# Up-projection remainders made by an adding DMA, and ten weight buffers of 1024 columns, in a one-core decoder layer

## The chip, the cores and the metric

The kernel runs on one core of one Trainium2 chip. Its time is the device time of one execution, in microseconds (us); the measure is the median over several runs. The engines are TensorE (PE; PEld is its weight loading), VectorE (DVE), ScalarE (ACT), GpSimd (POOL) and SyncE (SP). SP and ACT issue the DMAs of the kernel before.

## The reference

One decoder layer on a sequence of 512 tokens of width 1024, float32. `D_FF` is 2816, so the up-projection has 2 x 2816 columns.

```
cond = silu(c)
sh1, sc1, g1, sh2, sc2, g2 = split(cond @ ada_w + ada_b)
u = rms_norm(x, mix_pre_g) * (1 + sc1) + sh1
qk_raw, v, o_pre, gates, glu = split(u @ w_in)
qk = silu(causal_dwconv(qk_raw, 4 taps));  h = mlstm_chunkwise(q, k, v, gates)
h = rms_norm(h, ml_norm_g) * sigmoid(o_pre)
y = silu(layer_norm(causal_dwconv(a * sigmoid(gt), 31 taps)))        # a, gt = halves of glu
x = x + g1 * rms_norm(concat(h, y) @ w_out, mix_post_g)
u = rms_norm(x, ffn_pre_g) * (1 + sc2) + sh2
up = causal_dwconv(u @ ffn_up, 3 taps)                               # the stage of the change
a, gt = halves of up
x = x + g2 * rms_norm((silu(gt) * a) @ ffn_down, ffn_post_g)
```

## The kernel before

**Products in three matmuls.** TensorE multiplies in a rounded 32-bit format (`F32R`). To keep float32 accuracy every operand is split in two: `hi` is the value rounded to that format, `lo` the remainder `value - hi`. A product is then `hi*hi + hi*lo + lo*hi`, three matmuls into one PSUM bank (`mm3`, L210). For weights ScalarE writes `hi` (L191) and GpSimd, in some places VectorE, subtracts for `lo` (L192). This is `w_split`; `w_load` fetches 1024 KB of weights (128 partitions x 2048 columns) into one of two raw buffers (pool `raws`) and splits them in four pieces of 512 columns.

**Buffers.** The pieces lie in the pool `wpool`: 20 buffers of 128 x 512 (`WSLOTS = 20`), two for a piece, so ten pieces. A buffer is given out in turn and is free again when the last matmul that reads it is done.

**Stages in the order of the program.** The opening with the first GLU columns, summed up over eight parts of the input as they arrive (`w_part`, `glu_pass`); the rest of the GLU projection; the value and gate columns (`make_v0`); four attention heads with their projections (`qko`, `vo`), with the 31-tap convolution of the other branch on VectorE, ScalarE and GpSimd beside them; the output projection (`mixa`, `mixb`); the up-projection in 22 units of 2 x 128 columns (`up`); the down-projection in seven products of half size (`dn`, Strassen's way of making one product from seven).

**A unit of the up-projection.** 48 matmuls of 512 columns into two PSUM banks of a ring of four; then, per bank, ScalarE and VectorE apply the three taps (`conv3`), ScalarE the silu, VectorE the product `a * silu(gt)`, and for every second unit GpSimd forms sums and ScalarE and VectorE split the result for the down-projection. Beside it run, for 11 of the units, a 1024 KB load of a `w_down` tile `b`, four subtractions on it (VectorE and GpSimd in turn, `weight_sums`) and a 1024 KB store of the result (`spill_t`). The weights of units 0 and 1 are split by VectorE into another pool, those of units 2 and 3 by VectorE into `wpool`; the other 18 units, 4 to 21, go through `w_load` with GpSimd.

**What sets the order.** TensorE and SP execute in the order in which the program is written. For ScalarE, VectorE and GpSimd the build's scheduler picks an order by its own estimates of time; the opening, and the stretch between the output projection and the third up-projection unit, stand in program order on them too. Each engine works through its list in that order and waits where an operand or a buffer isn't ready.

Of the kernel before, what the change touches and what calls it, by code (L numbers as in the profile page):

```python
# [33 lines left out]

WARM = (3, 8, 8, 2)
CVS = 4
WSLOTS = 20
RAWS = 2


# [15 lines left out]
def decoder_layer(ctx, tc, w_glu0, x, c, adaT, vecs, w_glu, w_qko, w_v0, w_vo, w_out, w_up, w_down, out):  # L56
    nc = tc.nc
    V, S, G, PE = nc.vector, nc.scalar, nc.gpsimd, nc.tensor

    const = ctx.enter_context(tc.tile_pool(name="const", bufs=1))  # L60
    slots = ctx.enter_context(tc.tile_pool(name="slots", bufs=SLOTS))
# [120 lines left out]

    def w_split(src, name, pool=None, tag="w", eng=None):

        n = src.shape[1]
        pool = pool or wpool
        hi = pool.tile([P, T], F32R, tag=tag, name=f"{name}h")
        lo = pool.tile([P, T], F32R, tag=tag, name=f"{name}l")  # L190
        S.activation(hi[:, :n], src, AF.Copy)  # L191
        (eng or G).tensor_tensor(out=lo[:, :n], in0=src, in1=hi[:, :n].bitcast(F32), op=ALU.subtract)  # L192
        return hi, lo

    def w_load(view, name, pool=None, tag="w", eng=None):

        n = view.shape[1]
        r = raws.tile([P, 2048], F32, tag="raw", name=name)
        nc.sync.dma_start(r[:, :n], view)
        return [w_split(r[:, a : min(a + T, n)], f"{name}_{a}", pool, tag, eng) for a in range(0, n, T)]  # L200

    def blk(pieces, b):
        hi, lo = pieces[b // 4]
# [135 lines left out]
    rows0 = {}  # L339

    def w_rows(k):
        rows0[k] = adas.tile([P, D], F32, tag="ada", name=f"wglu0_{k}")
        nc.sync.dma_start(rows0[k][:, : G0 * P], w_glu0[k])

    def w_part(k, a, n):
        wk.append(w_split(rows0[k][:, a : a + n], f"wglu0_{k}_{a}"))

    def glu_pass(ps, i, p):
        a, b = ((0, 0), (1, 0), (0, 1))[p]
# [120 lines left out]
    def make_v0():  # L470

        n = DH + GB
        wv = []
        for q in range(0, KT, 4):
            r = raws.tile([P, 2048], F32, tag="raw", name=f"wv0_{q}")
            nc.sync.dma_start(r[:, : 4 * n], w_v0[q // 4])
            wv += [tuple(w[:, :n] for w in w_split(r[:, i * n : (i + 1) * n], f"wv0_{q + i}")) for i in range(4)]
        v_tile(0)
        banks = [mmbank(f"v0_{tt}") for tt in range(NT)]
        for tt, ps in enumerate(banks):  # L480
            ts = slice(tt * P, (tt + 1) * P)
            for k in range(KT):
                mm3(ps[:, :n], (u[k][0][:, ts], u[k][1][:, ts]), wv[k], k == 0, k == KT - 1)
            V.tensor_tensor(out=gz[:, tt, :], in0=ps[:, DH : DH + GB], in1=vcols("gate_b", 0, GB), op=ALU.add)
            S.activation(vs[0][tt][:, :DH], ps[:, :DH], AF.Copy)
# [526 lines left out]

    def up_split(i, r, pool, tag):
        q = len(up_w[i])
        up_w[i].append(w_split(r[:, q * T : (q + 1) * T], f"wup{i}_{q * T}", pool, tag, V))

    NE = 2
    early = []
# [12 lines left out]
            for k in range(KT):  # L1031
                mm3(ps[:, th * HT : (th + 1) * HT], blk(up_w[i], half * KT + k), (u2h[:, th, k, :], u2l[:, th, k, :]), k == 0, k == KT - 1)

    up_w = {0: w_load(w_up[0], "wup0", slots, "t", V)}
    raw1 = raw_up(1)
    send_rows(KT, 2 * KT, nc.sync)
    gs2r = row(1, cvtile, "gs2", nc.sync)
# [96 lines left out]
    for i in range(NF):  # L1134
        if i < NE:
            pa, pg = early[i]
        else:
            pieces = up_w.get(i) or w_load(w_up[i], f"wup{i}")
            if i in AT:
                weight_load(AT.index(i))  # L1140
            if i in (4, 8, 12, 16):
                ada_block(38 + i // 2, last_lo[0])
                ada_block(39 + i // 2, last_lo[0])
            if i == 19:
                ada_done(40, 48)
# [12 lines left out]
        anchor[0] = S.activation(g, g, AF.Silu)  # L1158
        if i % 2 == 0:
            x_, r_, *more = side_parts(f"f{i}") if i >= AT[-1] else [slot(f"f{q}{i}") for q in "xr"]  # L1160
        cs = slice(i % 2 * HT, (i % 2 + 1) * HT)
        V.tensor_tensor(out=x_[:, cs], in0=a[:, :HT], in1=g[:, :HT], op=ALU.mult)
        V.tensor_tensor(out=r_[:, cs], in0=a[:, HT:], in1=g[:, HT:], op=ALU.mult)
        if i % 2:
            y_, q_ = more or [slot(f"f{q}{i}") for q in "yq"]
            G.tensor_tensor(out=y_[:, :HT], in0=r_[:, :HT], in1=r_[:, HT:], op=ALU.add)
            G.tensor_tensor(out=y_[:, HT:], in0=y_[:, :HT], in1=x_[:, :HT], op=ALU.subtract)
            G.tensor_tensor(out=q_[:, :HT], in0=x_[:, :HT], in1=r_[:, :HT], op=ALU.subtract)
            G.tensor_tensor(out=q_[:, HT:], in0=x_[:, HT:], in1=y_[:, HT:], op=ALU.subtract)
            home = [None, None]  # L1170
            if i == NF - 1:
                ends = [adas.tile([P, D], F32R, tag="ada", name=f"f{q}{i}") for q in "xy"]
                home = [(z[:, :T], z[:, T:]) for z in ends]
            af.append(split_f(x_, f"fx{i}", i == 1, home[0]))
            asum.append(split_f(y_, f"fy{i}", i == 1, home[1]))
            j = i // 2
            nc.scalar.dma_start(spill["s34"][:, j * T : (j + 1) * T], q_)
            nc.scalar.dma_start(spill["a22"][:, j * HT : (j + 1) * HT], r_[:, HT:])
        if i - 1 in AT:
            weight_store(AT.index(i - 1))  # L1180
        if i in AT:
            weight_sums(AT.index(i))
# [10 lines left out]
    def product(weights, left, th, hf, name, js=range(JP), start=False, by_tile=JP):  # L1193

        late = []
        for a in range(js.start, js.stop, GJ):
            m = min(GJ, js.stop - a)
            turn_at = at[0] % (RAWS + len(rings))
            r = raws.tile([P, 2048], F32, tag="raw", name=f"{name}_{a}") if turn_at < RAWS else rings[turn_at - RAWS]
            at[0] += 1  # L1200
            nc.sync.dma_start(r[:, : m * T].rearrange("p (j n) -> p j n", j=m), weights(a, a + m))
            for n in range(m):
                j = a + n
                turn[0] += 1
                w = w_split(r[:, n * T : (n + 1) * T], f"{name}_{j}", eng=V if turn[0] % 2 else G)
                if j < by_tile:
                    for q in range(2):
                        piece(left(j), q, w, banks[2 * th + q][hf], start and j == 0, j == js.stop - 1)
                else:
                    late.append((j, w))  # L1210
        return late
# [167 lines left out]
```

## Time and profile before

| what | us |
|---|---|
| median of 3 runs (least, most) | 767.93 (767.7, 768.16) |
| profiled execution, span from first to last instruction | 767.4 |
| median less that span | 0.5 |

The profile is of one execution; it gives its span and no other time of its own. Granted TensorE clock over the span: 0.999 of full speed. A row of a group reads: line, engine, operation, written tile <- read tiles, shapes, count, then busy us and mean ns of one, then the idle time of the engine just before them with what ended it. A row of the timeline reads: start us, length us, then the instruction. Tile names in rows leave numbers out, so `wup_512l` is the remainder of the second piece of any unit, and `p_1l` that of the second piece of any of the down-projection's products.

### The profile page before, as it was taken

The numbers are of one execution on the slowest core, as the hardware profiler recorded it, in microseconds if no ns is written. First come the engines' busy times: TensorE is split into PE (matmuls) and PEld (weight loads), VectorE is DVE, ScalarE is ACT, GpSimd is POOL, SyncE is SP. The second block draws the span as 40 slices with busy tenths as digits, with TensorE's granted clock in tenths as the row PEclk, the third lists the DMA queues.
The fourth block names the chain that finished last, engine by engine and source line by source line (L and its number), as shares of the span: only waits on it lengthen the run. The fifth ranks groups of instructions, "written<-read, shape, count | busy, mean of one in ns | idle before, by whom it ended". The sixth has DMA issues, their size and how long they took to land.

```text
span 767.4 us, 10129 instructions
## 1 busy us (share of the span) xinstructions
PE 756.0 (99%) x3480; PEld 625.1 (81%) x3480; DVE 576.6 (75%) x837; ACT 410.7 (54%) x778; POOL 516.5 (67%) x428
## 2 busy tenths in 40 slices
PE   7999999999999999999999999999999999999996
PEld 5778898878788788888889988888888888888885
DVE  6669999979979696476989978675684775654547
ACT  6675428585665655573345444443534444566633
POOL 4779849796494872645631179786887884599943
PEclk9999999999999999999999999999999999999999
DMA  8973313411131241655965755666767565796273
GB/s 317 349 281 113 112 56 117 158 56 56 55 111 56 98 168 64 235 199 168 365 222 183 271 210 191 240 219 247 262 231 275 187 239 185 271 397 241 93 249 135
DMA packets 40136, 147.32 MB, mean 192 GB/s; under 512 B 3826, under 2 KB 5266, under 8 KB 30484
## 3 DMA queue, kind: packets, MB, share of 16 engines
q1 hardware_dynamic: 27524, 96.59, 34.9%
q10 hardware_dynamic: 12560, 50.08, 18.3%
q8 instruction: 27, 0.44, 0.2%
q14 instruction: 25, 0.20, 0.1%
HBM read 126.59 MB, written 20.07 MB: 191 GB/s over the span
## 4 chain that ended last, share of the span: by engine, by line
PE 93%; DMA 4%; POOL 1%; ACT 1%; issue 0%; DVEq 0%; SPq 0%; DVE 0%; POOLq 0%; ACTq 0%
PE up L210 31%; PE dn L210 13%; PE qko L210 13%; PE vo L210 9%; PE glu L210 7%; PE mixa L210 6%; PE mixb L210 6%; DMA wglu<-in_w_glu 3%; PE o L562 2%; PE s L551 2%; PE v L210 2%; PE glu L350 1%; DMA xn<-in_x 1%; PE xT L992 0%; PE hT L593 0%
## 5 line engine op out<-in xcount | busy, mean ns | idle before, releaser
L774 DVE SCALAR_TENSOR_TENSOR cv<-gt,cvw,cv 128x485 f32<-128x485 f32 (+24 forms) x200 | 137.2, 731 | 2.1 <-ACT cv L762 0.8
L770 POOL TENSOR_TENSOR cs<-cs,cs 128x510 f32<-128x510 f32 (+3 forms) x32 | 42.1, 1316 | 0.2
L192 POOL TENSOR_TENSOR wup_0l<-wup,wup_0h 128x512 fp32r<-128x512 f32 x18 | 25.0, 1389 | 19.4 <-ACT wup_0h L191 19.3
L210 PE MATMUL up<-u2h,wup_0h 128*128 128x512 f32 (+1 forms) x96 | 35.8, 373 | 0.0
L210 PE MATMUL up<-u2h,wup_0l 128*128 128x512 f32 (+1 forms) x96 | 35.7, 371 | 0.0
L210 PE MATMUL up<-u2h,wup_512h 128*128 128x512 f32 (+1 forms) x96 | 35.6, 371 | 0.0
L210 PE MATMUL up<-u2l,wup_512h 128*128 128x512 f32 (+1 forms) x96 | 35.6, 371 | 0.0
L210 PE MATMUL up<-u2h,wup_512l 128*128 128x512 f32 (+1 forms) x96 | 35.6, 371 | 0.0
L210 PE MATMUL up<-u2l,wup_0h 128*128 128x512 f32 (+1 forms) x96 | 35.6, 371 | 0.0
L210 PE MATMUL up<-u2h,wup_1024h 128*128 128x512 f32 (+1 forms) x92 | 35.0, 381 | 0.0
L210 PE MATMUL up<-u2l,wup_1024h 128*128 128x512 f32 (+1 forms) x92 | 34.9, 380 | 0.0
L210 PE MATMUL up<-u2h,wup_1536l 128*128 128x512 f32 (+1 forms) x92 | 34.9, 380 | 0.0
L210 PE MATMUL up<-u2h,wup_1536h 128*128 128x512 f32 (+1 forms) x92 | 34.9, 380 | 0.0
L210 PE MATMUL up<-u2l,wup_1536h 128*128 128x512 f32 (+1 forms) x92 | 34.9, 380 | 0.0
L210 PE MATMUL up<-u2h,wup_1024l 128*128 128x512 f32 (+1 forms) x92 | 34.9, 380 | 0.0
L176 DVE SCALAR_TENSOR_TENSOR junk<-ada,cb 128x1024 bf16<-128x1024 f32 x20 | 29.9, 1493 | 2.6 <-DMA ada<-in_adaT 2.5
L768 ACT ACTIVATE cs<-gt,cvw 128x511 f32<-128x511 f32 (+4 forms) x40 | 27.1, 713 | 6.1 <-POOL cs L770 3.5
L192 POOL TENSOR_TENSOR wup_1536l<-wup,wup_1536h 128x512 fp32r<-128x512 f32 x18 | 24.6, 1365 | 6.0 <-ACT wup_1536h L191 5.4
L191 ACT ACTIVATE wup_512h<-wup 128x512 fp32r<-128x512 f32 x22 | 13.8, 629 | 25.7 <-PE up L210 20.9
L192 POOL TENSOR_TENSOR wup_1024l<-wup,wup_1024h 128x512 fp32r<-128x512 f32 x18 | 23.6, 1314 | 5.0 <-ACT wup_1024h L191 5.0
L330 DVE SCALAR_TENSOR_TENSOR junk<-ada,cps 128x1024 bf16<-128x1024 f32 x16 | 19.5, 1220 | 9.8 <-DMA ada<-in_adaT 9.2
L1113 DVE TENSOR_TENSOR b<-b 128x512 f32<-128x512 f32 x11 | 19.4, 1762 | 8.6 <-POOL b L1112 8.6
(1097 smaller groups left out, 2726.8 us busy)
## 6 DMA issues: line engine op xcount, KB each, us to landing
wup<-in_w_up SPq DMA_DIRECT2D x22, 1024.0 KB, 5.0
b<-in_w_down ACTq DMA_DIRECT2D x11, 1024.0 KB, 5.1
spill_t<-b ACTq DMA_DIRECT2D x11, 1024.0 KB, 3.9
ada<-in_adaT ACTq DMA_DIRECT2D x20, 512.0 KB, 4.8
wqko<-in_w_qko SPq DMA_DIRECT2D x9, 1024.0 KB, 4.8
ada<-in_adaT SPq DMA_DIRECT2D x16, 512.0 KB, 7.5
wo<-in_w_out SPq DMA_DIRECT2D x8, 1024.0 KB, 5.5
wvo<-in_w_vo SPq DMA_DIRECT2D x6, 1024.0 KB, 4.8
```

Of the source, the lines that this page charges most:

```text
L176: t = V.scalar_tensor_tensor(out=junk, in0=r, scalar=1.0, in1=cb, op0=ALU.mult, op1=ALU.mult, accum_out=mod[:, i : i + 1])
L191: S.activation(hi[:, :n], src, AF.Copy)
L192: (eng or G).tensor_tensor(out=lo[:, :n], in0=src, in1=hi[:, :n].bitcast(F32), op=ALU.subtract)
L210: PE.matmul(ps, l, r, start=start and i == 0, stop=stop and i == 2, skip_group_check=again)
L330: V.scalar_tensor_tensor(out=junk, in0=first[k][:, i * D : (i + 1) * D], scalar=1.0, in1=cps, op0=ALU.mult, op1=ALU.mult, accum_out=part[: ...
L350: PE.matmul(ps, blk(wk, i)[a], u[k][b], start=k == 0 and p == 0, stop=k == KT - 1 and p == 1)
L551: PE.matmul(sp[:, :n], ks[d][:, cc * P : (cc + 1) * P], qs[d][:, cc * P :], start=d == 0, stop=d == 1)
L562: PE.matmul(o[:, : DH + 2], E[h][cc][:, a : a + P], vs[h][cc], start=cc == 0, stop=cc == tt)
L768: S.activation(t[:, d:], cvx[j][:, : T - d], AF.Copy, scale=w(CK - 1 - d))
L770: G.tensor_tensor(out=side[:, d:], in0=side[:, d:], in1=t[:, d:], op=ALU.add)
L774: tap = V.scalar_tensor_tensor(out=cp[:, d:], in0=cvx[j][:, : T - d], scalar=w(CK - 1 - d), in1=cp[:, d:], op0=ALU.mult, op1=ALU.add)
L1113: V.tensor_tensor(out=b22, in0=b22, in1=b11, op=ALU.subtract)
```

## The change

A remainder of units 4 to 21 is no longer subtracted by GpSimd. `w_load_added` takes the 2048 raw columns in two halves of 1024. For each half ScalarE rounds (L224 in the new file), VectorE writes the negated rounded part into the remainder's buffer (L225), and GpSimd issues a DMA that adds the raw weights onto that buffer (L226), `lo = -hi + w`. The buffers of `wpool` become ten of 128 x 1024, and all other users put two pieces side by side into one buffer (`pair`, `w_splits`); their subtractions stay with the engines that had them.

```diff
-WSLOTS = 20
+WSLOTS = 10
...
-    def w_split(src, name, pool=None, tag="w", eng=None):
-
-        n = src.shape[1]
+    def pair(name, pool=None, tag="w"):
+
         pool = pool or wpool
-        hi = pool.tile([P, T], F32R, tag=tag, name=f"{name}h")
-        lo = pool.tile([P, T], F32R, tag=tag, name=f"{name}l")
-        S.activation(hi[:, :n], src, AF.Copy)
-        (eng or G).tensor_tensor(out=lo[:, :n], in0=src, in1=hi[:, :n].bitcast(F32), op=ALU.subtract)
+        wide = 2 * T if pool is wpool else T
+        return [pool.tile([P, wide], F32R, tag=tag, name=f"{name}{z}") for z in "hl"]
+
+    def w_split(src, hi, lo, eng=None):
+
+        S.activation(hi, src, AF.Copy)
+        (eng or G).tensor_tensor(out=lo, in0=src, in1=hi.bitcast(F32), op=ALU.subtract)
         return hi, lo
 
+    def w_splits(src, name, pool=None, tag="w", eng=None, step=T):
+
+        n, out = src.shape[1], []
+        for a in range(0, n, step):
+            if pool or a % (2 * step) == 0:
+                hi, lo = pair(f"{name}_{a}", pool, tag)
+                at = 0
+            m = min(step, n - a)
+            out.append(w_split(src[:, a : a + m], hi[:, at : at + m], lo[:, at : at + m], eng(a // step) if eng else None))
+            at += step
+        return out
...
+    def w_load_added(view, name):
+
+        r = raws.tile([P, 2048], F32, tag="raw", name=name)
+        nc.sync.dma_start(r, view)
+        out = []
+        for a in range(0, 4 * T, 2 * T):
+            hi, lo = pair(f"{name}_{a}")
+            src = r[:, a : a + 2 * T]
+            S.activation(hi, src, AF.Copy)
+            V.tensor_scalar(out=lo, in0=hi.bitcast(F32), scalar1=-1.0, scalar2=None, op0=ALU.mult)
+            G.dma_start(lo.bitcast(F32), src, accum_op=ALU.add)
+            out += [(hi[:, b : b + T], lo[:, b : b + T]) for b in (0, T)]
+        return out
...
-            pieces = up_w.get(i) or w_load(w_up[i], f"wup{i}")
+            pieces = up_w.get(i) or w_load_added(w_up[i], f"wup{i}")
```

TensorE's and SP's lists keep their order. Three places of the other lists follow. GpSimd's around the weights of units 8 and 9 (`wup8`, `wup9`; `fy5` and `fq5` are the sums of unit 5, `b2` the third `w_down` tile); before:

```order
L192 TENSOR_TENSOR wup8_0l_4835<-wup8_4832,wup8_0h_4834 128x512
L192 TENSOR_TENSOR wup8_512l_4839<-wup8_4832,wup8_512h_4838 128x512
L192 TENSOR_TENSOR wup8_1024l_4843<-wup8_4832,wup8_1024h_4842 128x512
L1166 TENSOR_TENSOR fy5_4626<-fr4_4539 128x256
L1168 TENSOR_TENSOR fq5_4627<-fx4_4538,fr4_4539 128x256
L1167 TENSOR_TENSOR fy5_4626<-fy5_4626,fx4_4538 128x256
L192 TENSOR_TENSOR wup8_1536l_4847<-wup8_4832,wup8_1536h_4846 128x512
L1169 TENSOR_TENSOR fq5_4627<-fx4_4538,fy5_4626 128x256
L192 TENSOR_TENSOR wup9_0l_4925<-wup9_4922,wup9_0h_4924 128x512
L1112 TENSOR_TENSOR b2_4661<-b2_4661 128x512
```

and now:

```order
L226 DMA wup8_0l_4667<-wup8_4664 128x1024
L1204 TENSOR_TENSOR fy5_4470<-fr4_4389 128x256
L1206 TENSOR_TENSOR fq5_4471<-fx4_4388,fr4_4389 128x256
L1205 TENSOR_TENSOR fy5_4470<-fy5_4470,fx4_4388 128x256
L1207 TENSOR_TENSOR fq5_4471<-fx4_4388,fy5_4470 128x256
L226 DMA wup8_1024l_4672<-wup8_4664 128x1024
L226 DMA wup9_0l_4751<-wup9_4748 128x1024
L1150 TENSOR_TENSOR b2_4499<-b2_4499 128x512
```

Four subtractions of a unit became two DMA issues, each behind VectorE's negation. VectorE's list at the same place (`fa6c` and `fg6c` are the taps of unit 6, which empty its PSUM banks), before:

```order
L1131 TENSOR_TENSOR fx5l_4633<-fx4_4538,fx5h_4632 128x512
L1093 SCALAR_TENSOR_TENSOR fa6c_4713<-up6_0_4663,vec_111,fa6c_4713 128x511
L1131 TENSOR_TENSOR fy5l_4637<-fy5_4626,fy5h_4636 128x512
L1093 SCALAR_TENSOR_TENSOR fa6c_4713<-up6_0_4663,vec_111,fa6c_4713 128x510
L1111 TENSOR_TENSOR b2_4661<-b2_4661 128x512
L1093 SCALAR_TENSOR_TENSOR fg6c_4717<-up6_1_4688,vec_111,fg6c_4717 128x511
L1113 TENSOR_TENSOR b2_4661<-b2_4661 128x512
L1093 SCALAR_TENSOR_TENSOR fg6c_4717<-up6_1_4688,vec_111,fg6c_4717 128x510
```

and now:

```order
L1169 TENSOR_TENSOR fx5l_4477<-fx4_4388,fx5h_4476 128x512
L1131 SCALAR_TENSOR_TENSOR fa6c_4551<-up6_0_4501,vec_111,fa6c_4551 128x511
L1131 SCALAR_TENSOR_TENSOR fa6c_4551<-up6_0_4501,vec_111,fa6c_4551 128x510
L225 TENSOR_SCALAR wup8_1024l_4672<-wup8_1024h_4671 128x1024
L1169 TENSOR_TENSOR fy5l_4481<-fy5_4470,fy5h_4480 128x512
L225 TENSOR_SCALAR wup9_0l_4751<-wup9_0h_4750 128x1024
L1149 TENSOR_TENSOR b2_4499<-b2_4499 128x512
L1131 SCALAR_TENSOR_TENSOR fg6c_4555<-up6_1_4526,vec_111,fg6c_4555 128x511
L1131 SCALAR_TENSOR_TENSOR fg6c_4555<-up6_1_4526,vec_111,fg6c_4555 128x510
L1151 TENSOR_TENSOR b2_4499<-b2_4499 128x512
```

Two negations of 1024 columns stand between the taps. ScalarE's list at the end of the opening (`gt0` is the tanh of a GLU gate, whose PSUM bank comes free with VectorE's product behind it), before:

```order
L191 ACTIVATE wglu3_0h_625<-wglu3_623 128x512
L191 ACTIVATE wglu3_512h_629<-wglu3_623 128x512
L438 ACTIVATE gt0_616<-glu1_248 128x512
L191 ACTIVATE wglu3_1024h_633<-wglu3_623 128x512
L438 ACTIVATE gt0_616<-glu3_250 128x512
```

and now:

```order
L174 DMA ada_17_2951<-in_adaT 128x1024
L193 ACTIVATE wglu3_0h_609<-wglu3_607 128x512 x2
L193 ACTIVATE wglu3_1024h_615<-wglu3_607 128x512 x2
L471 ACTIVATE gt0_600<-glu1_248 128x512
L471 ACTIVATE gt0_600<-glu3_250 128x512
```

All four roundings of the unit stand ahead of the first tanh.

More of the change, by code (lines that the diff above doesn't have):

```diff
@@ L199, in w_load @@
         nc.sync.dma_start(r[:, :n], view)
-        return [w_split(r[:, a : min(a + T, n)], f"{name}_{a}", pool, tag, eng) for a in range(0, n, T)]
+        return w_splits(r[:, :n], name, pool, tag, eng)
+    def w_load_added(view, name):
[10 more added lines that the diff above has]
+        return out
     def blk(pieces, b):
@@ L343, in w_rows @@
         nc.sync.dma_start(rows0[k][:, : G0 * P], w_glu0[k])
+    kept0 = {}
     def w_part(k, a, n):
-        wk.append(w_split(rows0[k][:, a : a + n], f"wglu0_{k}_{a}"))
+        if a == 0:
+            kept0[k] = pair(f"wglu0_{k}")
+        hi, lo = (z[:, a : a + n] for z in kept0[k])
+        wk.append(w_split(rows0[k][:, a : a + n], hi, lo))
     def glu_pass(ps, i, p):
@@ L476, in make_v0 @@
             nc.sync.dma_start(r[:, : 4 * n], w_v0[q // 4])
-            wv += [tuple(w[:, :n] for w in w_split(r[:, i * n : (i + 1) * n], f"wv0_{q + i}")) for i in range(4)]
+            wv += w_splits(r[:, : 4 * n], f"wv0_{q}", step=n)
         v_tile(0)
@@ L1014, in up_split @@
         q = len(up_w[i])
-        up_w[i].append(w_split(r[:, q * T : (q + 1) * T], f"wup{i}_{q * T}", pool, tag, V))
+        if tag == "t" or q % 2 == 0:
+            up_pair[0] = pair(f"wup{i}_{q * T}", pool if tag == "t" else None, tag)
+        at = q % 2 * T if tag != "t" else 0
+        up_w[i].append(w_split(r[:, q * T : (q + 1) * T], *(z[:, at : at + T] for z in up_pair[0]), V))
+    up_pair = [None]
     NE = 2
@@ L1032, in up_half @@
                 mm3(ps[:, th * HT : (th + 1) * HT], blk(up_w[i], half * KT + k), (u2h[:, th, k, :], u2l[:, th, k, :]), k == 0, k == KT - 1)
-    up_w = {0: w_load(w_up[0], "wup0", slots, "t", V)}
+    up_w = {0: w_load(w_up[0], "wup0", slots, "t", lambda n: V)}
     raw1 = raw_up(1)
@@ L1201, in product @@
             nc.sync.dma_start(r[:, : m * T].rearrange("p (j n) -> p j n", j=m), weights(a, a + m))
-            for n in range(m):
+            first_turn = turn[0]
+            turn[0] += m
+            for n, w in enumerate(w_splits(r[:, : m * T], f"{name}_{a}", eng=lambda n: G if (first_turn + n) % 2 else V)):
                 j = a + n
-                turn[0] += 1
-                w = w_split(r[:, n * T : (n + 1) * T], f"{name}_{j}", eng=V if turn[0] % 2 else G)
                 if j < by_tile:
```

## The prediction

> **What bounds the kernel now.** I read the page first, then the chain in order of time, then what TensorE waited for. The first fence is from the page: the span, TensorE's busy line, and the chain that ended last by engine and by line.
>
> ```profile
> span 767.4 us, 10129 instructions
> PE 756.0 (99%) x3480; PEld 625.1 (81%) x3480; DVE 576.6 (75%) x837; ACT 410.7 (54%) x778; POOL 516.5 (67%) x428
> ...
> PE 93%; DMA 4%; POOL 1%; ACT 1%; issue 0%; DVEq 0%; SPq 0%; DVE 0%; POOLq 0%; ACTq 0%
> PE up L210 31%; PE dn L210 13%; PE qko L210 13%; PE vo L210 9%; PE glu L210 7%; PE mixa L210 6%; PE mixb L210 6%; DMA wglu<-in_w_glu 3%; PE o L562 2%; PE s L551 2%; PE v L210 2%; PE glu L350 1%; DMA xn<-in_x 1%; PE xT L992 0%; PE hT L593 0%
> ```
>
> The same chain by time (start, length, what), three of its pieces:
>
> ```profile
> 51.18 54.40 PE glu L210 x240
> ...
> 421.49 212.81 PE up L210 x984
> ...
> 656.22 102.24 PE dn L210 x450
> ```
>
> And all the waits of TensorE in the run (total, times, longest):
>
> ```profile
> PE cps L159 <- ACT crow L158: 2.9, 1, 2.9
> PE glu L350 <- ACT uh L371: 1.3, 1, 1.3
> PE glu L350 <- ACT uh L405: 0.9, 1, 0.9
> ```
>
> From 51 us to the end of the down-projection at 758.5 us the chain is TensorE alone, and its only waits lie before. 240 matmuls in 54.40 us make 226.7 ns each, so one unit of the up-projection (48 matmuls) takes 10.9 us and one 1024-column pair of weights (24 matmuls) 5.44 us. The change leaves TensorE's list of matmuls as it is. So whatever VectorE, ScalarE or GpSimd save in the up-projection is worth nothing to the end. The question is only whether the new way of making the remainders can make TensorE wait.
>
> **What the change removes.** GpSimd's 72 subtractions of units 4 to 21:
>
> ```profile
> L192 POOL TENSOR_TENSOR wup_0l<-wup,wup_0h 128x512 fp32r<-128x512 f32 x18 | 25.0, 1389 | 19.4 <-ACT wup_0h L191 19.3
> ...
> L192 POOL TENSOR_TENSOR wup_1536l<-wup,wup_1536h 128x512 fp32r<-128x512 f32 x18 | 24.6, 1365 | 6.0 <-ACT wup_1536h L191 5.4 <-PE up L210 0.5
> L192 POOL TENSOR_TENSOR wup_512l<-wup,wup_512h 128x512 fp32r<-128x512 f32 x18 | 24.3, 1348 | 0.9 <-ACT wup_512h L191 0.9
> ...
> L192 POOL TENSOR_TENSOR wup_1024l<-wup,wup_1024h 128x512 fp32r<-128x512 f32 x18 | 23.6, 1314 | 5.0 <-ACT wup_1024h L191 5.0
> ```
>
> That is 25.0 + 24.6 + 24.3 + 23.6 = 97.5 us of GpSimd. They are hidden behind TensorE with a large margin. Unit 8's first remainder and the matmul that reads it (start, length):
>
> ```profile
> 480.31 1.29 POOL L192 TENSOR_TENSOR wup_0l<-wup,wup_0h 128x512 fp32r<-128x512 f32 x1
> ...
> 504.03 0.39 PE L210 MATMUL up<-u2h,wup_0l 128*128 128x512 f32 x1
> ```
>
> It is ready at 481.6 us and read at 504.0 us, 22 us later. Gain: 0.
>
> **What it adds on the engines.** Per 1024 columns one rounding on ScalarE instead of two, one negation on VectorE, one DMA issue on GpSimd. The nearest rows (ns: least, median, most):
>
> ```profile
> L191 ACT ACTIVATE wup_0h<-wup x22: 615/632/634, 387.5 to 621.2; 128x512 fp32r<-128x512 f32 x22
> L192 DVE TENSOR_TENSOR wup_0l<-wup,wup_0h x4: 679/687/692, 388.6 to 427.6; 128x512 fp32r<-128x512 f32 x4
> L260 DVE TENSOR_SCALAR xn<-xn,xs x3: 478/480/487, 6.9 to 10.2; 128x512 f32<-128x512 f32 x3
> ```
>
> ScalarE: at most 2 x 0.63 = 1.26 us a pair, as before. VectorE: between 2 x 0.48 = 0.96 and 2 x 0.69 = 1.38 us; I take 0.96, since the row of 0.48 is the same operation. 36 of them are 35 us (up to 50). What covers them is shown by the stretch from the first of these remainders to the use of the last (busy us of PE, PEld, DVE, ACT, POOL, then clock, DMA share, GB/s):
>
> ```profile
> 436.00:651.00 215.00, 215.00 (x950) 177.96 (x949) 149.09 (x178) 97.19 (x158) 164.80 (x138) 1.00 0.63 227
> ```
>
> VectorE goes from 149 to 184 of 215 us (199 at the high end), GpSimd from 165 to 67 plus the issues. Behind a negation that waits for its rounding stand VectorE's two taps that empty PSUM; four banks are two units, and a bank is written again 1.5 units (16 us) after it was finished, so a delay of some us there costs nothing. Without that cover each late tap would be TensorE's wait. Cost: 0.
>
> **What it adds on the DMA engines.** 36 transfers of 512 KB, 18.9 MB, in those 215 us, on a queue of GpSimd's that the trace does not have. What the engines do there now (packets, MB, share of 16 engines):
>
> ```profile
> DMA packets 10022, 48.75 MB, mean 227 GB/s; under 512 B 1032, under 2 KB 2320, under 8 KB 5008
> ...
> q10 hardware_dynamic: 6558, 29.09, 37.0%
> q1 hardware_dynamic: 3450, 19.48, 25.6%
> ```
>
> 62.6% of 215 us is 134.6 us; 80 us are free. The price of an add is bounded from rows of plain transfers. Median us from issue to landing:
>
> ```profile
> spill_t<-b ACTq DMA_DIRECT2D x11, 1024.0 KB, 3.9
> ...
> wup<-in_w_up SPq DMA_DIRECT2D x22, 1024.0 KB, 5.0
> ...
> x1d<-x SPq DMA_DIRECT2D x8, 256.0 KB, 2.1
> ...
> spare<-in_adaT ACTq DMA_DIRECT2D x12, 512.0 KB, 8.3
> ```
>
> From 2.1 us for 256 KB and 3.9 us for 1024 KB, 768 KB more take 1.8 us, or 1.2 us for 512 KB on idle engines. Queue q1 has 25.6% of 215 us = 55.0 us for 19.48 MB, or 1.48 us for 512 KB among other traffic. If an add costs what a copy costs, 36 take 43 to 53 us. But an add has two operands to fetch, the weights and the negated rounded part, for each word that it stores. If the fetching sets the pace it costs two copies, 86 to 107 us. That the two fetches overlap would be the low end; the far end is the slowest plain 512 KB row, 8.3 us to landing, and 36 x 8.3 = 299 us, but that row is of loads that queued behind each other, and I keep it only as a sign that the upper side is open. I take two copies, since a second operand is a second transfer in kind, the middle 96 us: 134.6 + 96 = 231 us of DMA work in 215 us. Cost: +16 us (86 gives +6, 107 gives +26).
>
> The Trainium skill, "Collectives: The Full Stack", section on the bandwidth ceiling and why AG, RS and AR differ, says that an adding transfer issues two reads per chunk on the same ring and halves its rate, 62.28 against 32.35 GB/s, a ratio of 1.93. By that the sum would be 134.6 + 1.93 x (43 to 53), an estimate of +3 to +22 us; no run here shows it yet.
>
> **Waits that change.** SP's weight loads waited for GpSimd's last subtraction of a unit; now they wait for the landing of its second add. Two raw buffers, so one load per 21.8 us and buffer: a load (5.0), rounding (1.3), negation (1.0) and two landings must fit, so a landing up to about 7 us is free, against 2.4 to 4 us on idle engines (1.2 or 2 x 1.2 for the bytes, and the 1.5 us that a transfer of no size would take by the two rows). Also the five pairs of buffers give 4 x 5.44 = 21.8 us from release to use, as much as the margin now. Late next, if the DMA engines fill, are the loads of w_down, since VectorE already waits for them in its queue:
>
> ```profile
> DVE b L1111 <- DMA b<-in_w_down: 9.9, 4, 4.1
> ```
>
> **Buffers of 1024 columns in the other stages.** The capacity is the same, but a pair comes free only with its second half, and roundings are grouped by pairs. Two places have less than 2 us of margin. At 51 us (start, length):
>
> ```profile
> 48.28 0.62 ACT L191 ACTIVATE wglu_512h<-wglu 128x512 fp32r<-128x512 f32 x1
> 49.40 0.60 ACT L438 ACTIVATE gt<-glu 128x512 f32<-128x512 f32 x1 [0.50 <-PE glu L350]
> ...
> 50.03 0.69 DVE L440 SCALAR_TENSOR_TENSOR gt<-gt,glu 128x512 f32<-128x512 f32 x1 [2.28 <-ACT gt L438]
> ...
> 51.02 0.39 PE L210 MATMUL glu<-uh,wglu_0h 128*128 128x512 f32 x1
> ```
>
> Now two more roundings at 0.52 us spacing stand ahead of the tanh, which then starts at 48.28 + 3 x 0.52 = 49.84 instead of 49.40. VectorE frees the bank at 50.72 + 0.44 = 51.16 us, and TensorE needs it at 51.02: +0.2 us. In the down-projection's last product:
>
> ```profile
> 744.52 1.30 POOL L192 TENSOR_TENSOR p_1l<-p,p_1h 128x512 fp32r<-128x512 f32 x1 [8.03 <-ACT p_1h L191]
> ...
> 747.63 0.39 PE L210 MATMUL dn<-p_1l,a_0h 128*128 128x512 f32 x1
> ```
>
> 1.8 us are left. The order ahead of it delays the put that frees the gain rows, and so SP's load, by one rounding, 0.6 us at most: 0. The coarser grain costs this stage one piece of lookahead (six matmuls, 1.4 us), less than these margins. The sum is 767.4 (span) + 16 + 0.2 = 783.6; the median of the runs shown lies 0.5 us above the span, so 784 us.
>
> **Rivals.** Within 0.2% (1.5 us) is about what a measurement of this kernel can tell from no change.
>
> *The adds fit.* An add costs a copy: 134.6 + 43 to 53 = 178 to 188 of 215 us, TensorE never waits, and the run ends at 767.9 + 0.2 = 768.1 us. It decides from (215 - 134.6) / 36 = 2.23 us of engine time an add, that is 1.5 to 1.9 copies. For it: the margin of 22 us, and idle DMA time in most slices. Against it: the second operand. The Trainium skill, "DMA: Bandwidth & Descriptors", section on the anatomy of a DMA issued by GpSimd, gives 2.0 us plus bytes over 436 GB/s for one such transfer, without an add; by that (an estimate of 1.2 us of data time each) this rival would hold.
>
> *The adds are slow.* Three copies' price (129 to 160 us) gives 264 to 295 of 215 us, +49 to +80, so 817 to 848 us; four pass 860. For it: queue and operation are unknown here, and 8.3 us rows exist. Landings above 7 us would also stretch the load loop.
>
> *A grain wait elsewhere.* The 1.8 us above, or a bank emptied late in a reordered stretch: +1.6 to 3 us, 770 to 771 us. Against it: the two places above are the tightest that I found.
>
> *Faster* would need a shorter opening (before 51 us) or ending, and neither loses work.
>
> **Chances.** Two copies 0.40, slow adds 0.20, a grain wait 0.05: slower 0.65. The adds fit: same 0.32. Faster 0.03. The forecast's own range is 773.5 to 794; the range for 8 in 10 takes in the fitting case from below and the nearer half of the slow one: 767 to 832.
>
> **What would show it.** In the changed profile: TensorE idle only between 460 us (unit 4, four units before 504) and 656 us, with waits on a DMA of a wup remainder; DMA share from 0.63 towards 0.9 or more there; a third queue of about 19 MB (a multiple of that if fetches are counted) and its landing time, 2.7 us if an add is a copy, 4 us and more if it is two. VectorE at 0.85 of the stretch. If instead no wait of TensorE names a wup remainder and the chain stays unbroken, the price of the add was wrong. If the waits stand before 436 or after 656 us, the grain was.

## The result, and the profile after

The changed kernel takes 815.19 us (median of 6 runs, 813.94 to 818.99), the kernel before beside it 767.96 us: a ratio of 1.062, 95% interval 1.060 to 1.065, or +47 us where +16 was forecast. The profiled execution of the changed kernel is the slowest of the six, 818.99 us, with a span of 817.3 us.

Its waits of TensorE (total, times, longest) were three rows before, all ahead of 51 us. Now:

```profile
PE up L238 <- DMA wup_0l<-wup: 14.1, 7, 3.8
PE up L238 <- DVE fg9c L1131: 5.0, 1, 5.0
PE up L238 <- DVE fg7c L1131: 4.1, 1, 4.1
PE up L238 <- DVE fg15c L1131: 3.4, 1, 3.4
PE dn L238 <- DVE gTs L727: 3.3, 1, 3.3
...
PE dn L238 <- POOL p_0l L194: 1.6, 2, 1.0
```

14.1 us is the wait for a remainder that a DMA makes, as forecast. Nearly as much, 12.5 us, is for `fg9c`, `fg7c` and `fg15c`: VectorE's convolution taps, whose end frees a PSUM bank.

The row of the stretch 436 to 651 us (busy us of PE, PEld, DVE, ACT, POOL, clock, DMA share, GB/s), which the prediction showed of before, and the DMA queues in it (packets, MB, share of 16 engines):

```profile
436.00:651.00 215.00, 190.32 (x790) 153.07 (x789) 118.80 (x170) 70.70 (x93) 79.81 (x81) 0.95 0.89 253
```

```profile
q0 software_dynamic: 4249, 15.51, 37.4%
q10 hardware_dynamic: 5440, 23.99, 29.9%
q1 hardware_dynamic: 2027, 14.72, 21.5%
```

The DMA engines went from 0.63 to 0.89 busy and not to 1, while TensorE stood still for a part of the time. Over the whole run the new queue has 18.88 MB:

```profile
q0 software_dynamic: 5184, 18.88, 12.0%
```

12.0% of 817.3 us is 98.1 us, or 2.72 us of engine time for each of 36 adds. The prediction took 96 us. So that price was right and the loss is three times what was made of it. The issues of the page (count, KB each, median us to landing) show what else changed: a load of weights 7.3 us where it was 5.0, a `w_down` tile 10.0 where it was 5.1, a store 7.8 where it was 3.9.

```profile
wup<-in_w_up SPq DMA_DIRECT2D x22, 1024.0 KB, 7.3
b<-in_w_down ACTq DMA_DIRECT2D x11, 1024.0 KB, 10.0
spill_t<-b ACTq DMA_DIRECT2D x11, 1024.0 KB, 7.8
...
wup_0l<-wup POOLq DMA_DIRECT2D x18, 512.0 KB, 8.3
wup_1024l<-wup POOLq DMA_DIRECT2D x18, 512.0 KB, 8.4
```

**The loop of the raw buffers.** One turn of a raw buffer, followed through the timeline of four engines (start, length): the load of unit 9 is issued, ScalarE rounds the first half, then the second, VectorE negates, GpSimd issues the second add, and SyncE issues the load of unit 11 into the same buffer.

```profile
494.06 0.33 SPq L219 DMA_DIRECT2D wup<-in_w_up  x1
...
505.27 1.06 ACT L224 ACTIVATE wup_0h<-wup 128x1024 fp32r<-128x1024 f32 x1 [6.43 <-DMA wup<-in_w_up]
...
509.19 0.63 ACT L1196 ACTIVATE fg6c<-fg6c 128x512 f32<-128x512 f32 x1 [2.19 <-DVE fg6c L1131]
...
509.73 1.05 ACT L224 ACTIVATE wup_1024h<-wup 128x1024 fp32r<-128x1024 f32 x1
...
512.05 0.68 DVE L225 TENSOR_SCALAR wup_1024l<-wup_1024h 128x1024 fp32r<-128x1024 f32 x1
...
513.14 0.90 POOL L226 DMA_DIRECT2D wup_1024l<-wup  x1 [1.30 <-DVE wup_1024l L225]
...
522.65 0.33 SPq L219 DMA_DIRECT2D wup<-in_w_up  x1
```

11.2 us to the first rounding, 4.5 to the second (it stands behind the gate's silu), 3.4 to the issue, 9.5 until SyncE can go on: 28.6 us. To keep TensorE's pace a raw buffer must come round every 21.8 us. The 18 loads start from 426.5 to 666.4 us, 14.1 us apart on average, where TensorE takes a unit in 10.9.

**The chain through `w_down`'s tiles.** The chain that ended last, by time, goes on from there over VectorE's queue:

```profile
506.97 0.68 DVE b L1149
507.65 0.67 DVE fg6c L1131
...
509.27 10.78 DMA b<-in_w_down
520.08 0.70 DVE b L1149
...
520.86 1.26 POOL b L1150
522.15 0.69 DVE b L1151
522.84 0.67 DVE fg7c L1131
...
524.43 7.01 PE up L238 x23
```

ScalarE issues the load of `b` behind the silu of `fg6c`; it lands 10.8 us later; VectorE's first subtraction has waited for it, and the taps of `fg7c`, which free the bank that TensorE waits for, stand behind that in VectorE's queue. The silu of `fg7c` and the next load stand behind those taps. DMA of `b` is 7.2% of the whole chain that ended last, 59 us, the largest share of any one transfer; it was not among the entries of before. The transfers of the raw buffers' loop stand in the same chain too: the loads `wup` with 4.7%, the adds with some 5%.

**Taps stand behind both.** VectorE's waits in 460 to 680 us are longer for roundings, most of which come late with a raw buffer's load, than for `b`:

```profile
DVE wup_0l L225 <- ACT wup_0h L224: 62.5, 9, 13.4
DVE b L1149 <- DMA b<-in_w_down: 22.0, 6, 6.2
```

TensorE's longest wait, for `fg9c`, is of the first kind (ScalarE, VectorE twice, TensorE):

```profile
551.01 1.06 ACT L224 ACTIVATE wup_0h<-wup 128x1024 fp32r<-128x1024 f32 x1 [13.89 <-DMA wup<-in_w_up]
552.10 0.69 DVE L225 TENSOR_SCALAR wup_0l<-wup_0h 128x1024 fp32r<-128x1024 f32 x1 [13.41 <-ACT wup_0h L224]
552.76 1.53 DVE L1131 SCALAR_TENSOR_TENSOR fg9c<-up,vec,fg9c 128x511 f32<-128x511 f32 x2
554.44 0.76 PE L238 MATMUL up<-u2h,wup_1024h 128*128 128x512 f32 x1 [5.01 <-DVE fg9c L1131]
```

The taps stand behind a negation that waited 13.4 us for its rounding; ahead of `fg15c` it waited 12.1 us, there because the rounding itself waited for a weight buffer that TensorE still read. Of the 12.5 us that TensorE waited for these three taps only the 4.1 of `fg7c` stand right behind a `b`.

### The profile page after: what moved, and what is told of

Its sections match the earlier page's. It is cut to its first block, busy times and chain, and to the rows that moved or that the text cites. A ratio compares the mean times of both kernels' runs of the same rounds, so it can differ in the third digit from the quotient of the medians.

```text
span 817.3 us, 10069 instructions
## 1 busy us (share of the span) xinstructions
PE 773.2 (95%) x3480; PEld 632.5 (77%) x3480; DVE 574.5 (70%) x873; ACT 401.0 (49%) x742; POOL 457.6 (56%) x392
## 3 DMA queue, kind: packets, MB, share of 16 engines
q0 software_dynamic: 5184, 18.88, 12.0%
## 4 chain that ended last, share of the span: by engine, by line
PE 59%; DMA 24%; DVE 7%; POOL 3%; ACT 3%; issue 3%; ACTq 0%; DVEq 0%; POOLq 0%; SPq 0%
PE qko L238 12%; PE dn L238 11%; PE vo L238 8%; DMA b<-in_w_down 7%; PE glu L238 7%; PE mixa L238 5%; DMA wup<-in_w_up 5%; PE up L238 4%; PE mixb L238 3%; DMA wup_1024l<-wup 3%; PE o L595 2%; PE s L584 2%; DMA ada<-in_adaT 2%; DMA wup_0l<-wup 2%; DMA wglu<-in_w_glu 2%
## 5 line engine op out<-in xcount | busy, mean ns | idle before, releaser
L807 DVE SCALAR_TENSOR_TENSOR cv<-gt,cvw,cv 128x485 f32<-128x485 f32 (+23 forms) x200 | 137.2, 730 | 1.3
L238 PE MATMUL up<-u2h,wup_0l 128*128 128x512 f32 (+1 forms) x176 | 69.5, 395 | 14.1 <-DMA wup_0l<-wup 14.1
L238 PE MATMUL up<-u2h,wup_1024h 128*128 128x512 f32 (+1 forms) x172 | 68.7, 399 | 13.7 <-DVE fg9c L1131 5.0
L238 PE MATMUL up<-u2h,wup_0h 128*128 128x512 f32 (+1 forms) x176 | 69.2, 393 | 0.7 <-DVE fa8c L1131 0.7
L226 POOL DMA_DIRECT2D wup_0l<-wup x18 | 15.9, 886 | 94.3 <-DVE wup_0l L225 91.8
L224 ACT ACTIVATE wup_0h<-wup 128x1024 fp32r<-128x1024 f32 x18 | 19.0, 1056 | 82.0 <-DMA wup<-in_w_up 65.8
L225 DVE TENSOR_SCALAR wup_0l<-wup_0h 128x1024 fp32r<-128x1024 f32 x18 | 13.7, 764 | 63.3 <-ACT wup_0h L224 63.3
L238 PEld LDWEIGHTS up<-u2h,wup_0l 128*128 128x128 f32 x176 | 34.3, 195 | 23.6 <-DMA wup_0l<-wup 17.1
L238 PEld LDWEIGHTS up<-u2h,wup_1024h 128*128 128x128 f32 x172 | 33.7, 196 | 22.4 <-issue 15.7
L238 PEld LDWEIGHTS up<-u2h,wup_0h 128*128 128x128 f32 x176 | 34.2, 194 | 7.6 <-ACT fg8c L1129 1.1
L238 PEld LDWEIGHTS up<-u2l,wup_0h 128*128 128x128 f32 x176 | 34.4, 195 | 6.8
L238 PEld LDWEIGHTS up<-u2h,wup_1024l 128*128 128x128 f32 x172 | 33.4, 194 | 6.9
L238 PEld LDWEIGHTS up<-u2l,wup_1024h 128*128 128x128 f32 x172 | 33.6, 195 | 6.6
```

Of the source, the lines that this page charges most:

```text
L224: S.activation(hi, src, AF.Copy)
L225: V.tensor_scalar(out=lo, in0=hi.bitcast(F32), scalar1=-1.0, scalar2=None, op0=ALU.mult)
L226: G.dma_start(lo.bitcast(F32), src, accum_op=ALU.add)
L238: PE.matmul(ps, l, r, start=start and i == 0, stop=stop and i == 2, skip_group_check=again)
L807: tap = V.scalar_tensor_tensor(out=cp[:, d:], in0=cvx[j][:, : T - d], scalar=w(CK - 1 - d), in1=cp[:, d:], op0=ALU.mult, op1=ALU.add)
```

## The experiments

Three theories were put up, then told apart. A: the engines' time for the transfers, 231 us in 215, is the loss. B: the loop of the raw buffers, and that of the five pairs of weight buffers, became longer than TensorE's pace. C: the chain through the landing of `b` and VectorE's queue. Rival besides: the coarser buffers.

**Buffers alone.**

```
-            pieces = up_w.get(i) or w_load_added(w_up[i], f"wup{i}")
+            pieces = up_w.get(i) or w_load(w_up[i], f"wup{i}")
```

> Leaves the DMA adds out: all 22 units make their remainder by a subtraction, with the ten buffers of 1024 columns kept. Theory A (DMA engines full: the adds' own time on the 16 engines, 2.7 us each, fills the stage): 768 us, no DMA wait on TensorE. Theory B (the loop of the two raw buffers: a buffer is held from its load to the landing of its second add, 28 us for two units where TensorE takes 21.8): 768 us too. Rival C (the coarser buffers cost something by themselves): 772 us or more.

768.33 us, ratio 1.0005 (0.9994 to 1.0017). The coarser buffers cost nothing; the whole loss is the adds'.

**An eighth of the bytes.**

```
-            G.dma_start(lo.bitcast(F32), src, accum_op=ALU.add)
+            G.dma_start(lo[:, :P].bitcast(F32), src[:, :P], accum_op=ALU.add)
```

> The DMA adds only 128 of the 1024 columns, so 7/8 of the remainder stays the negated rounded part; every instruction, queue and wait stays in its place, with an eighth of the bytes. Theory A: 12 us of engine time in all, 768 us. Theory B: the path from ScalarE over VectorE and GpSimd's queue to the landing stays, but the landing falls to some 2.5 to 3.5 us and the loads to 5: 768 to 772 us. If the hops over the engines' queues alone were too long: 775 us or more.

768.90 us, 1.0006 (0.9996 to 1.0016; one of the ten runs took 4382 us and is not in the ratio). Seven eighths of the remainder are left out; an add of what is left takes a median of 4.0 us to land. The hops over three engines and GpSimd's issue are hidden. A and B said so both.

**A copy in place of the add.**

```
-            G.dma_start(lo.bitcast(F32), src, accum_op=ALU.add)
+            G.dma_start(lo.bitcast(F32), src)
```

> The add becomes a plain copy of the same 512 KB by the same queue, from the same place in the program, so the remainder holds the raw weights and not the difference. Theory A: if the accumulation is what makes 2.7 us, the third queue falls to about 1.4 us each (49 us in all), the stage then has 184 us of transfers in 215: 768 to 772 us. Theory B: landings shorten from 8.3 to some 4 to 5 us, loads from 7.4 to 5, the loop of two raw buffers from 28 to about 22 us: 768 to 775 us. If the issue by GpSimd and not the accumulation costs: still 2.7 us each and 800 to 820 us.

The remainder holds raw weights here. 786.91 us, 1.023 (1.020 to 1.027). Its queue in the page:

```profile
q0 software_dynamic: 5184, 18.88, 6.1%
```

6.1% of 784.6 us is 47.9 us, 1.33 us for each, so an add costs 2.05 copies of engine time. But all three expected times were missed: 134.6 + 48 = 183 us in 215 is no excess, and 18 us were lost. First evidence against A as the whole.

**Half of the units.**

```
+            pieces = up_w.get(i) or (w_load_added if i % 2 else w_load)(w_up[i], f"wup{i}")
```

> Only the nine odd units of 5 to 21 use the adds; the even ones subtract. Theory A: 18 adds of 2.7 us, 49 us, 184 us of transfers in 215: 768 to 772 us. Theory B: only every second raw buffer turn is lengthened, a pair of turns takes about (28 + 22)/2 = 25 us of two units against 21.8: about 775 to 795 us.

787.86 us, 1.026 (1.024 to 1.028), with a DMA share of 0.78 in 436 to 651 us. A is wrong here too: 184 us of transfers, and about 19 us lost.

**The adds read from HBM.**

```
-            G.dma_start(lo.bitcast(F32), src, accum_op=ALU.add)
+            G.dma_start(lo, view[:, a : a + 2 * T].bitcast(F32R), accum_op=ALU.add)
```

> The add reads the weights a second time from HBM in place of the raw buffer, so a raw buffer is free as soon as ScalarE has read it; number, size and queue of the adds are the same. Theory A (engines full): the third queue keeps its 2.7 us each, DMA share 0.9 or more, 810 to 825 us. Theory B (raw loop): loads run ahead again, TensorE does not wait, 768 to 785 us.

802.87 us, 1.045 (1.043 to 1.046): between the two expectations. SyncE no longer waits for an add's landing, and that gives back 12 of 47 us. What carries the rest is told by the chain of this kernel from 480 to 600 us:

```profile
by line: DMA b<-in_w_down 49.7%; DMA spill_t<-b 18.0%; issue 11.7%; POOL b L1150 4.1%; DVE wup_0l L225 2.3%; DVE b L1151 1.7%; DVE fg8c L1131 1.2%; DVE fg4c L1131 1.2%; DVE fg10c L1131 1.2%; DVE fg12c L1131 1.2%; DVE fg6c L1131 1.2%; DVE fg
```

(The view ends the line there.) Two thirds of it are loads and stores of `b`. VectorE's wait for `b` in 460 to 680 us, 22.0 us in the changed kernel, grew:

```profile
DVE b L1149 <- DMA b<-in_w_down: 64.9, 11, 12.3
```

This is where theory C came from.

**As much time on the DMA engines, with nobody waiting.**

```
-            V.tensor_scalar(out=lo, in0=hi.bitcast(F32), scalar1=-1.0, scalar2=None, op0=ALU.mult)
-            G.dma_start(lo.bitcast(F32), src, accum_op=ALU.add)
+            G.tensor_tensor(out=lo, in0=src, in1=hi.bitcast(F32), op=ALU.subtract)
+            for z in range(2):
+                nc.sync.dma_start(apart[4 * int(name[3:]) + 2 * (a > 0) + z], view[:, a : a + 2 * T])
```

> The remainders are made by a subtraction on GpSimd again (1024 columns at a time), and beside them 72 copies of 512 KB go from HBM to an unused place in HBM, two for each pair of buffers, on SyncE's queue; nothing waits for them. Theory A (engines full): the copies take 72 x 1.3 us or more, as much as the 36 adds, so the time is that of the adds, 800 to 820 us. Theory B (loops: the landing of an add stands in the loop of the two raw buffers and in that of the five pairs, and both became longer than what TensorE takes for as many units): the same traffic outside the loops only lengthens the loads from 5 to 8 to 10 us, 768 to 775 us.

803.13 us, 1.046 (1.044 to 1.047), as A said, but not in the way of A:

```profile
436.00:651.00 215.00, 209.98 (x915) 171.93 (x914) 120.47 (x156) 84.20 (x110) 137.87 (x87) 0.99 0.99 368
```

With the DMA engines at 0.99 TensorE lost 5 us in this stretch. 25.0 us are one wait at the start of the down-projection; its chain goes back over the last load of `b`, which ScalarE issued only after rounding a down-projection load that came late on the queue of the copies. The copies had 1.45 us each (q1 rose from 267.8 to 372.4 us of engine time), 104 us in all, somewhat more than the adds' 98.1, for twice their bytes. The test is not clean, since its backlog comes due at one place; what it shows is that engines at 0.99 need not hold up the up-projection.

**The negation on ScalarE.**

```
-            V.tensor_scalar(out=lo, in0=hi.bitcast(F32), scalar1=-1.0, scalar2=None, op0=ALU.mult)
+            S.activation(lo, src, AF.Copy, scale=-1.0)
```

> The negated rounded part is written by ScalarE from the raw weights (scale -1) in place of VectorE from the rounded ones; the adds stay as they are. It takes one hop and VectorE's queue out of both loops (0.7 us of work and 1 to 10 us of waiting for each pair) and gives ScalarE 1.05 us more for each pair. Theory A: 815 us. Theory B: the loop of the raw buffers falls from 28 to some 26 us for two units: 798 to 808 us.

807.55 us is the median of four runs: 797.82, 804.77, 810.32 and 811.63. The ratio 1.043 (1.037 to 1.049) is that of the two shorter ones alone, whose median is 801.3 us. The spread is too wide to tell what one hop less gives.

**Without the `w_down` sums.** The calls of `weight_load`, `weight_store` and `weight_sums` are left out.

> Leaves the sums of the down-projection's weights out (11 loads and 11 stores of 1 MB, and their subtractions on VectorE and GpSimd); the down-projection reads the plain weights in their place, as many bytes. The 36 adds stay. Theory A: 231 us of transfers less some 53 leave 178 in 215: 768 to 772 us. Theory B: with fewer transfers beside them an add lands in 5 to 6 us and a load in 5 to 6, which brings the loop of the raw buffers to about 22 us: 768 to 785 us. Both are right if it is 768; over 785 us the waits on the engines' queues would be the larger part.

768.69 us, 1.0003 (0.9993 to 1.0013). All 36 adds are there and TensorE never waits for one. An add lands in a median of 5.3 us, a load in 6.1. Both theories were right, so it told only that the two kinds of transfers hurt together. The next two separate the bytes of `b` from the waits for it.

**The transfers of `b` kept, its subtractions left out.**

```
-        if i in AT:
-            weight_sums(AT.index(i))
```

> Every transfer of the changed kernel stays (36 adds, 18 loads, 11 loads and 11 stores of the down-projection's weights), only the four subtractions for each of those 11 are left out, so VectorE and GpSimd no longer stand in their queues until such a load has landed; the weights are stored as they came. Theory A (transfers alone: 231 us of engine time in 215): 815 us. Theory B (the loop of the two raw buffers alone: 28 us for two units): 805 to 815 us. Theory C (a chain through the queues: VectorE waits for the landing of b, behind it stand the convolution taps, behind them ScalarE's gate and the issue of the next load): 780 to 797 us, with what the transfers' sum costs left over.

804.96 us, 1.048 (1.043 to 1.053). 10 us of 47 come back. The raw buffers carry this one: ScalarE's wait for the loads in 460 to 680 us is

```profile
ACT wup_0h L224 <- DMA wup<-in_w_up: 99.9, 12, 13.0
```

63.9 us it was in the changed kernel. TensorE still waits 7.2 us for taps here, though no tap stands behind a `b`. B's number fits; C alone is out.

**Both at once:** the adds from HBM, and no subtractions of `b`.

> Both at once: the adds read the weights from HBM (no raw buffer held until a landing), and the four subtractions for each of the 11 down-projection weights are left out; the bytes of all transfers stay. What remains is the transfers' own sum, 231 to 237 us in 215, and the loop of the five pairs of buffers. Theory A alone: 800 to 815 us. Theories B and C together: 784 to 794 us, DMA share over 0.95. A time at 768 us would say that the transfers' sum is smaller than the stage.

769.35 us, 1.0012 (1.0000 to 1.0024). Expected were 784 to 794 for B and C together, with the transfers' sum left over. The row of the stretch, all of TensorE's waits from 400 us on,

```profile
436.00:651.00 215.00, 214.28 (x944) 176.53 (x943) 115.07 (x184) 86.73 (x117) 62.97 (x76) 1.00 1.01 309
```

```profile
PE up L238 <- DMA wup_0l<-in_w_up: 0.7, 1, 0.7
```

and the queues in that stretch:

```profile
q0 software_dynamic: 5184, 18.88, 44.5%
q10 hardware_dynamic: 6366, 28.43, 33.6%
q1 hardware_dynamic: 3361, 18.88, 22.2%
```

Every byte and all 36 adds are there (2.66 us of engine time each, so reading from HBM made them no cheaper to speak of); only the subtractions of `b` are missing. The DMA engines are full, an add lands in a median of 12.6 us, longer than in the changed kernel, and TensorE waits 0.7 us. So A falls: the stage has room for these transfers, with nothing to spare. One cut gives 12 us, the other 10, both together 46: two chains side by side, each of which alone holds the stage back. As shown, with the raw buffers' loop opened the wait for `b` grew from 22.0 to 64.9 us, and without the subtractions that for the loads from 63.9 to 99.9.

**Half of the units, from HBM.** The edits of those two kernels together.

> Adds in the nine odd units only, and these read the weights from HBM, so that a raw buffer is free when ScalarE or GpSimd has read it. 184 us of transfers in 215, as with the raw buffers' adds in nine units (787.9 us). Theory B (raw buffers): 768 to 772 us. Theory C (the chain by the landing of b): 775 to 787 us. Theory A: 768 us, but that already failed at nine units with raw buffers.

800.51 us, 1.041 (1.037 to 1.045), and missed by all: 13 us slower than the same nine units from the raw buffers. VectorE's waits in 460 to 680 us say by what:

```profile
DVE b L1149 <- DMA b<-in_w_down: 62.7, 10, 14.0
```

47.0 us it was with the raw buffers. A `wup` load takes a median of 7.1 us here against 5.7 there. So opening one loop can lengthen the other chain; that the loads, which start earlier, crowd the loads of `b` was not tested by itself.

**Five units that have no `b`.**

```
+            pieces = up_w.get(i) or (w_load_added if i in (5, 8, 11, 14, 17) else w_load)(w_up[i], f"wup{i}")
```

> Adds in the five units 5, 8, 11, 14 and 17 only, those that have no load of the down-projection's weights. Ten adds of 2.7 us, 27 us: 162 us of transfers in 215. All theories: 768 to 771 us if an add's landing only lengthens the chain where a load of b or another add stands beside it; over 775 us each add costs 0.7 us or more wherever it stands.

778.15 us, 1.012 (1.009 to 1.015): not the 768 to 771 us of all theories but the other case named, over 775, with 0.9 us for each of ten adds. VectorE's wait for `b` in 436 to 660 us rose from 9.9 us to

```profile
DVE b L1149 <- DMA b<-in_w_down: 38.4, 8, 8.1
```

Units without a `b` have neighbours that load or store one.

**Only the place in VectorE's queue.** The first subtraction of `b` is ordered behind the gate's products of its unit; all work stays.

```
-        V.tensor_tensor(out=r_[:, cs], in0=a[:, HT:], in1=g[:, HT:], op=ALU.mult)
+        gated[0] = V.tensor_tensor(out=r_[:, cs], in0=a[:, HT:], in1=g[:, HT:], op=ALU.mult)
...
-        V.tensor_tensor(out=b11, in0=b12, in1=b11, op=ALU.subtract)
+        behind(V.tensor_tensor(out=b11, in0=b12, in1=b11, op=ALU.subtract), gated[0])
```

> All work and all transfers as in the changed kernel; the first subtraction of each down-projection weight is ordered on VectorE behind the gate's products of the same unit, so that the taps, ScalarE's gate and the issue of the next load no longer stand behind its landing. Only one of the two chains is cut, the raw buffers are still held until an add has landed. Two chains in parallel (theories B and C both): 798 to 812 us, as without the subtractions (805.0). Theory C alone: 768 to 785 us. Theory A: 815 us.

802.88 us, 1.045 (1.042 to 1.048), as without the subtractions.

**The same place, and the adds from HBM.**

> The same order on VectorE, and the adds read the weights from HBM, so that no raw buffer waits for an add's landing; all work, all 36 adds and all bytes stay. Both chains cut: 768 to 780 us, DMA share near 1. If leaving the subtractions out had helped by something else than their place in the queue: 795 us or more.

781.27 us, 1.015 (1.013 to 1.018), 1 us above the expected range. With all work and all bytes, moving one subtraction in a queue and reading the adds' source from elsewhere gives back 34 of 47 us, more than the sum of the two alone (12 each). The DMA share in 436 to 651 us is 0.97. No wait of TensorE names a tap any more; in the up-projection it waits for adds alone, 9.0 us:

```profile
PE up L238 <- DMA wup_1024l<-in_w_up: 5.6, 5, 2.5
PE up L238 <- DMA wup_0l<-in_w_up: 3.4, 3, 1.5
```

VectorE's waits for `b` are still there in 460 to 680 us:

```profile
DVE b L1149 <- DMA b<-in_w_down: 42.4, 8, 10.6
```

For one of the adds the trace leads back to them: VectorE waits 10.1 us for `b` until 541.35, GpSimd's next subtraction of it and its sums follow, then ScalarE's rounding at 546.12, the negation at 547.83 and the add's issue at 548.92; it lands 12.5 us later, and TensorE has waited 1.5 us for it. That `b` makes up the whole of the 12 us that are left was not shown.

No version is faster than the kernel before: TensorE's own work is the bound there, and the adds take nothing off it.

## Why the prediction was right or wrong

**What bounds, and the removed subtractions: right.** All that counted was whether TensorE has to wait; without the adds, the new buffers give 768.33 us. The 0.2 us at 51 us cannot be told from nothing (its own numbers, 51.16 less 51.02, give 0.14), and no wait of TensorE in the changed kernel names that bank.

**The price of an add on the engines: right.** 96 us taken, 98.1 us measured, and 2.05 times a copy. That the second operand's fetch is the reason no run shows. The Trainium skill, "Collectives: The Full Stack", section on the bandwidth ceiling, has a ratio of 1.93 for the adding transfers of a collective; 2.05 here is 6% above it. The rival that an add costs a copy falls; so does, as a forecast of this kernel, the rule of the Trainium skill, "DMA: Bandwidth & Descriptors", section on the anatomy of a DMA issued by GpSimd: 2.0 us plus bytes over 436 GB/s makes an estimate of 3.2 us. The fastest plain copy landed in 2.9 us, but the median was 5.6 beside the other transfers.

**"134.6 + 96 = 231 us of DMA work in 215 us. Cost: +16 us": wrong as a step.** The excess of a sum over a window was taken as the loss. The run with both chains cut (adds from HBM, no subtractions of `b`) shows that this charge is about 1 us: all 18.88 MB of the adds went through in those 215 us, in 44.5% or 95.7 us, and the other two queues took 33.6 + 22.2 = 55.8%, 120 us, for 47.3 MB, where before they took 134.6 us for 48.6 MB. So 134.6 was not a sum of work that the adds come on top of. The true part of the step, that the engines get full, is what makes each landing longer.

**"So a landing up to about 7 us is free": the term that was mis-sized.** The landing was 8.3 us, little above 7, but the other terms grew with it: the load 7.3 (11.2 in the turn shown, the wait for its landing included) for 5.0, and 4.5 us between the two roundings, which the sum did not hold at all since ScalarE's queue was left out. It gave 2.4 to 4 us for a landing on idle engines where its terms, 1.2 + 1.5, begin at 2.7. And it counted two landings one behind the other, where only the second stands in the turn (9.5 us from its issue until SyncE goes on). 28.6 us came for 21.8. The prediction knew this as its rival of slow adds, but tied it to three copies' price.

**"A delay of some us there costs nothing" (VectorE's taps): wrong in the size of the delay.** 5.0, 4.1 and 3.4 us of TensorE's waits end with such a tap. The place was named, a negation that waits for its rounding with the taps behind it, and the cover of 16 us was there; but the wait was 13.4 us ahead of `fg9c`, whose taps ended at 554.3 us for a bank that TensorE had finished at 531.7, 22.6 us after and not 16. For `b` the prediction named the loads of `w_down` as late next and stopped there; behind that wait stand the taps too (`fg7c`), behind them the silu, behind it the next load. VectorE's busy share, 0.85 forecast, fell to 0.55 (118.80 of 215): it waited.

**Where and how it would show: partly.** TensorE stops first near 509 us and the waits end with the down-projection's first weights; they name a remainder, as forecast, in 14.1 of 33.5 us. The range to 832 us held the time.

Of the 49.9 us of span 33.5 are TensorE's waits in these stages (the six rows above and three of 1.1, 0.7 and 0.2 us). Some 10 us more are a slower TensorE behind them, below. The remaining 6 us were not followed.

## What to carry to other kernels

Before a transfer replaces an engine's operation, walk the loop in which its landing will stand, with the landings that full DMA engines give and with every in-order queue on the way, and compare the turn with the bound engine's pace; the sum of transfer time against the window is not that test. Look also for waits on a DMA that already stand in a queue ahead of work for the bound engine: they have no price until transfers slow down. When taking out one suspect gives back little, take out two together before dismissing either: here 12 and 10 us alone were 46 us together.

## What the runs showed of the hardware

TensorE comes back slowly from a long wait. Of the changed kernel, the stretch with a 4.05 us wait, the start after it and a later one (clock and DMA share are the last but two and last but one numbers):

```profile
521.00:523.00 2.00, 0.00 (x0) 0.00 (x0) 0.85 (x2) 0.00 (x0) 1.20 (x2) 1.00 0.04 8
525.00:527.00 2.00, 2.00 (x6) 1.61 (x5) 0.89 (x3) 0.80 (x3) 1.47 (x3) 0.50 1.00 381
529.00:531.00 2.00, 2.00 (x10) 1.68 (x9) 2.00 (x4) 1.05 (x2) 1.04 (x2) 1.00 1.06 293
```

```profile
524.99 0.63 PE L238 MATMUL up<-u2l,wup_1024h 128*128 128x512 f32 x1
525.42 0.63 PE L238 MATMUL up<-u2h,wup_1024l 128*128 128x512 f32 x1
```

The granted clock is 0.50 there, and matmuls start 0.43 us apart instead of 0.227, for some 3 us. All seven waits of TensorE from 3.05 to 5.01 us in these stages are followed so, the four from 1.05 to 1.38 us are not. From 460 us on, the trace of the changed kernel has 51 steps of 0.36 to 0.50 us between 512-column matmuls where that of before has none: 51 x 0.2 = some 10 us, an estimate. The Trainium skill, "TensorE: Matmul & The Clock Gate", Part 1, has the array at half rate after an idle window of about 3.4 us and back after as long a busy one; this wait and the 3 us behind it agree; here waits of 3.05 to 3.26 us were followed by it too.

Busy time of a queue is not a fixed price of its bytes: as above, the same kind of transfers took 2.54 us of engine time per MB with the engines full and 2.77 before. And an add of 64 KB took 0.55 us (2.6% of 766.9 us over 36), not an eighth of 2.72; it had as many packets, 144, as the one of 512 KB.
